# A two-layer decoder trunk in fp32: in the second layer's attention, the copies of a head's transposed probabilities and its value product come one head later, and ScalarE writes the longer high parts

## The chip, the cores and the metric

The kernel runs on one core of a Trainium2 chip. Five engines work side by side, each through its own queue in order: TensorE (PE in the profile, its weight loads apart as PEld), VectorE (DVE), ScalarE (ACT), GpSimd (POOL) and SyncE (SP), which issues the DMAs. The metric is the device time of one launch in microseconds; smaller is better. Beside the timed runs there is one profiled execution, from which all rows of the profile come.

## The reference, cut to what matters

512 positions with 1024 features pass through two layers, each an attention mixer and a squared-ReLU MLP. The change lies in the mixer of the second layer, the forgetting attention with 16 heads of 64 features:

```python
def fox_mixer(h, w_in, b_forget, w_out):
    q, k, v, fz = _split(h @ w_in, ODD_SPLITS)      # 16 heads x 64 each, and 16 forget logits
    log_f = jax.nn.log_sigmoid(fz + b_forget)
    cum = jnp.cumsum(log_f, axis=1).transpose(0, 2, 1)
    def block(c):                                   # 128 queries
        s = einsum('bhqd,bhkd->bhqk', qc, k) * scale + cq[..., None] - cum[:, :, None, :]
        p = masked_softmax(s, key_pos[None, :] <= t[:, None])
        return einsum('bhqk,bhkd->bhqd', p, v)
    ...
    return o @ w_out
```

All of it is in float32. Each head has four query blocks of 128 rows; block qi sees 128 x (qi + 1) keys.

## The kernel before, in words

**Products.** TensorE works on numbers in two parts: a high part in a rounded float32 format and a low part, the rest. A product of two such numbers takes three matmuls (`mm3`, lines 129 to 131: high by high, high by low, low by high). For every loaded piece of a weight, ACT writes the high part into the tile `whl` (line 91) and DVE or POOL subtracts it from the raw weight (line 94). A string of letters, `FOX_LOW`, tells for each piece of this stage which of the two engines subtracts: 34 letters, D for DVE, P for POOL.

**The stage.** `fox` runs through a written list of steps:

```python
FOX_ORDER = "v0 f k0 k1 k2 k3 p0 v1 k4 p1 p2 o01 k5 v3 v2 p3 k6 p4 p5 p6 k7 o23 o45 p7 o67"
```

`v` computes the values of four heads, `f` the sums of the forget logits, `k3` the queries and keys of pair 3 (heads 6 and 7), `p3` the attention of this pair, `o23` the output projection of pairs 2 and 3 with the addition to the residual stream. The list is the order in which the program is written. The order on each engine comes from a scheduler that plays the program through with modelled durations; work in a priority block (`self.prio()`) is taken ahead of work written earlier. A pool with n buffers lets a tile begin only when the tile n places before it was read to the end. Accumulators have two buffers for each name: `acc` for projections, `s` for logits, `o` for value products.

**Queries and keys.** A projection of 128 columns serves two heads and lies in `acc`. For each head ACT copies the query or key (lines 1259 and 1262), DVE computes the low part straight from `acc` (402 and 400) and POOL rounds a copy (406). The buffer of `acc` is free when both heads of the pair have been read out.

**One head in `softmax_t`.** The blocks are taken in two halves, first queries 3 and 2, then 1 and 0. For each block TensorE makes the logits (line 457, two matmuls), DVE adds the mask and takes the row's bound (461), ACT takes the exponent and its row sum (462). For each half DVE computes the two scales of its rows (464, 465). Then the scaled probabilities are written as float16 into the tile `HL`, the high part by POOL (472) and the low part by DVE (473), in pieces of 384 and 128 columns (query 3), 384 (query 2), 256 and 128 (queries 1 and 0). SP issues one transposing DMA from `HL` to `HT` (475). ACT copies the high half of `HT` into `PTh` (479) and POOL the low half into `PTl` (through `round`, 406). TensorE multiplies with the values (`pv`, 489 and 490), and `combine` scales the result into one half of the pair's tile `o` (ACT at 499, DVE at 500). After both heads of a pair POOL splits `o` into two parts `O` (`split_o`, 406 and 505). The output projection works on the two pairs' `O` (129 to 131), and DVE adds each of its eight accumulators to the residual (520).

**Buffers.** The probabilities `P` have three (`fP`), `HL` two, `HT` one, `PTh` and `PTl` two each.

The functions as they stand before the change:

Of the kernel before, what the change touches and what calls it, by code (L numbers as in the profile page):

```python
# [7 lines left out]
F32 = mybir.dt.float32  # L8
# [3 lines left out]
AF = mybir.ActivationFunctionType  # L12
ALU = mybir.AluOpType
AX = mybir.AxisListType

P = 128
S = 512
D = 1024
NT = S // P
# [8 lines left out]
P_UP = 32768.0  # L28
# [20 lines left out]
class Trunk:  # L49
# [395 lines left out]
    def softmax_t(self, passes, band):  # L445


        nc = self.nc
        pt = self.pP.tile([P, PTW], F32, tag="P", name=self.nm("P"))
        st = self.sm.tile([P, 3, 4], F32, tag="sst", name=self.nm("sst"))  # L450
        hl = self.pHL.tile([P, 2, PTW], F16, tag="HL", name=self.nm("HL"))
        for q0 in (2, 0):
            for qi in (q0 + 1, q0):
                w = P * (qi + 1)
                ps = self.psum("s")
                for i, (q, k) in enumerate(passes):
                    nc.tensor.matmul(ps[:, :w], q[:, qi * P:(qi + 1) * P], k[:, :w],
                                     start=i == 0, stop=i == len(passes) - 1)
                seg = pt[:, SEG[qi]:SEG[qi] + w]
                mn, sm = (st[:, a, qi:qi + 1] for a in range(2))  # L460
                nc.vector.tensor_tensor_reduce(seg, ps[:, :w], band[:, S - w:S], 1.0, 3e38, ALU.add, ALU.min, mn)
                nc.scalar.activation(seg, seg, AF.Exp, bias=mn, scale=-1.0, accum_out=sm)
            r = st[:, 2, q0:q0 + 2]
            nc.vector.reciprocal(r, st[:, 1, q0:q0 + 2])
            nc.vector.tensor_scalar(r, r, P_UP, None, op0=ALU.mult)
            for qi in (q0 + 1, q0):
                r = st[:, 2, qi:qi + 1]
                parts = [(0, min(qi + 1, 3), qi * P)] + ([(3, 4, PTOFF[3])] if qi == 3 else [])
                for j0, j1, off in parts:
                    seg = pt[:, SEG[qi] + j0 * P:SEG[qi] + j1 * P].rearrange("p (j c) -> p j c", c=P)  # L470
                    view = lambda a: hl[:, a, off:].rearrange("p (j c) -> p j c", c=P)[:, 0:3 * (j1 - j0 - 1) + 1:3, :]
                    nc.gpsimd.tensor_scalar(view(0), seg, r, 1.0, op0=ALU.mult, op1=ALU.mult)
                    nc.vector.scalar_tensor_tensor(view(1), seg, r, view(0), op0=ALU.mult, op1=ALU.subtract)  # L473
        t = self.pHT.tile([P, 2 * PTW // P, P], F16, tag="HT", name=self.nm("HT"))
        nc.sync.dma_start_transpose(t, hl.rearrange("p a b -> p (a b)"))
        tv = t.rearrange("p (a b) c -> p a (b c)", a=2)
        hi = self.pPT.tile([P, PTW], FR, tag="PTh", name=self.nm("PTh"))
        lo = self.pPT.tile([P, PTW], FR, tag="PTl", name=self.nm("PTl"))
        nc.scalar.activation(hi, tv[:, 0], AF.Copy)
        self.round(lo, tv[:, 1])  # L480
        return hi, lo

    def pv(self, po, pt, vs, first, last):
# [688 lines left out]
    def fox(self, hs):  # L1172
        self.phase, self.pieces = FOX_LOW, 0
        nc, I = self.nc, self.I
        w = I["odd_w_in"][0]
        wo = I["odd_w_out"][0]
        lo, hi = slice(0, HD), slice(HD, P)
        with ExitStack() as cx:
            pool = lambda name, bufs: cx.enter_context(self.tc.tile_pool(name=name, bufs=bufs))
            self.pP = pool("fP", 3)  # L1180
            self.pPT = pool("fPT", 2)
            self.pHL = pool("fHL", 2)
            self.pHT = pool("fHT", 1)
            o2 = pool("fo", 2)
            a1 = cx.enter_context(self.tc.tile_pool(name="attf1", bufs=1))
            wv = self.cols(w, [(2048, 2304), (3072, 3088)])
# [2 lines left out]
            band = a1.tile([P, S], F32, name="mband")  # L1189
# [7 lines left out]
            V = [a1.tile([P, 16, 2, HD], FR, tag=f"v{t}", name=f"v{t}") for t in range(NT)]  # L1197

            def values(c):

                wc = wv if c == 0 else self.cols(w, [(2048 + 256 * c, 2304 + 256 * c)])
                for t in range(NT):
                    ps = self.psum("acc")
                    self.proj_n(ps, wc, 272 if c == 0 else 256, x, t)
                    if c == 0:
                        nc.vector.tensor_copy(zt[:, t], ps[:, 256:272])
                    dst = V[t][:, 4 * c:4 * c + 4]
                    with self.tc.high_priority(offset=0):
                        pv = ps[:, :256].rearrange("p (h d) -> p h d", h=4)
                        nc.scalar.activation(dst[:, :, 0, :], pv, AF.Copy)  # L1210
                        self.sub(dst[:, :, 1, :], pv, dst[:, :, 0, :])
# [30 lines left out]
            def qk(i):  # L1242
                wc = self.cols(w, [(128 * i, 128 * i + 128)])
                psq = self.psum("acc")
                self.proj_t(psq, wc, 0, x)
                wc = self.cols(w, [(1024 + 128 * i, 1024 + 128 + 128 * i)])
                psk = self.psum("acc")
                self.proj_t(psk, wc, 0, x)
                st = []
                for j, r in enumerate((lo, hi)):  # L1250
                    head = 2 * i + j
                    q1 = pq.tile([P, S], FR, tag="Q1", name=self.nm("Q1"))
                    q2 = pq.tile([68, S], FR, tag="Q2", name=self.nm("Q2"))
                    k1 = pq.tile([P, S], FR, tag="K1", name=self.nm("K1"))
                    k2 = pq.tile([68, S], FR, tag="K2", name=self.nm("K2"))
                    nc.sync.dma_start(q2[64:68].bitcast(F32), fd[head, 0:4])
                    nc.sync.dma_start(k2[64:68].bitcast(F32), fd[head, 4:8])
                    with self.tc.high_priority(offset=0):
                        nc.scalar.activation(q1[lo], psq[r], AF.Copy, scale=-SCALE)
                        self.round(q2[lo], q1[lo].bitcast(F32))  # L1260
                        self.sub(q1[hi], psq[r], q1[lo], -SCALE)
                        nc.scalar.activation(k1[lo], psk[r], AF.Copy)
                        self.round(k1[hi], k1[lo].bitcast(F32))
                        self.sub(k2[lo], psk[r], k1[lo])
                    st.append((q1, k1, q2, k2))
                return st

            def pair(i, st):
                o = o2.tile([P, S], F32, tag="o", name=self.nm("o"))
                for j in range(2):  # L1270
                    head = 2 * i + j
                    q1, k1, q2, k2 = st[j]
                    with self.prio():
                        pt = self.softmax_t([(q1, k1), (q2, k2)], band)
                        po = self.psum("o")
                        self.pv(po, pt, [self.flat(V[t][:, head]) for t in range(NT)], True, True)
                        self.combine(po, o, j == 0, 1.0 / P_UP)
                return self.split_o(o)

            st, o = {}, {}  # L1280

            def step(op, arg):
                if op == "v":
                    values(int(arg))
                elif op == "f":
                    forget()
                elif op == "k":
                    st[int(arg)] = qk(int(arg))
                elif op == "p":
                    o[int(arg)] = pair(int(arg), st[int(arg)])  # L1290
                elif op == "o":
                    pairs = [int(a) for a in arg]
                    self.out_proj(wo, pairs, [o[a] for a in pairs], hs)

            for s in FOX_ORDER.split():
                step(s[0], s[1:])
# [41 lines left out]
```

## Time and profile before

| | us |
|---|---|
| median of 3 runs | 1250.22 (1249.81 to 1255.96) |
| the profiled execution | 1252.43 |
| its span, first to last instruction | 1250.7 |
| PE busy | 1207.5 (97%) |
| PEld busy | 1015.8 (81%) |
| DVE busy | 989.8 (79%) |
| ACT busy | 652.2 (52%) |
| POOL busy | 505.2 (40%) |
| mean granted clock of TensorE | 0.986 of full speed |

The first mixer runs to about 290 us, the first MLP to 635, the forgetting attention to 900, and the second MLP to the end. How to read the rows: a group is a line, an engine, an operation and output<-inputs with their shapes, then the count, the busy time and the mean of one in ns, and the idle time just ahead of them with what ended it. A wait is put down to the instruction or DMA that came last. A row of windows gives the length, then for PE, PEld, DVE, ACT and POOL the busy time, then the clock that TensorE was granted, the busy share of the DMA engines and their GB/s. The chain of waits goes back from the last instruction to what released each step; a row of it has its start, its length and the instruction.

### The profile page before, as it was taken

To read this page: it belongs to the slowest core of one execution; us is meant where nothing else is said; L and a number is where in the kernel's file an instruction comes from. 1 tells how busy PE (TensorE), PEld (TensorE's weight loads), DVE (VectorE), ACT (ScalarE), POOL (GpSimd) and SP (SyncE) were. 2 spreads that over 40 slices of the span, in tenths; PEclk is the share of its full clock that TensorE was granted. 3 is DMA by queue.
4 is the path that set the end of the run, shared out by engine and by line. 5 is a ranking of instruction groups with operands and counts; after the bars stand their busy time and mean duration, and the time that the engine had idled before them with its cause. 6 is when DMAs were issued, how large, how long until landed. Compare 5 with 4: busy or idle time off the path is not lost.

```text
span 1250.7 us, 16964 instructions
## 1 busy us (share of the span) xinstructions
PE 1207.5 (97%) x6055; PEld 1015.8 (81%) x6055; DVE 989.8 (79%) x1683; ACT 652.2 (52%) x1163; POOL 505.2 (40%) x518
## 2 busy tenths in 40 slices
PE   9999999999999999999999898897899999999997
PEld 7889987888888888888887786886698888888886
DVE  7877778788887898789776788649587897789875
ACT  6447656774645445544345565455365445444542
POOL 3435466642533323332015756445335233332314
PEclk9999999999999999999999999998899999999999
DMA  8952232223333333332044554534454224333301
GB/s 243 338 158 55 81 116 71 62 91 98 111 113 101 106 95 103 114 105 82 5 111 110 131 116 94 128 105 83 137 144 125 85 85 135 101 90 96 101 1 68
DMA packets 183440, 134.25 MB, mean 107 GB/s; under 512 B 47875, under 2 KB 158635, under 8 KB 183356
## 3 DMA queue, kind: packets, MB, share of 16 engines
q1 hardware_dynamic: 183196, 132.94, 37.9%
q8 instruction: 48, 0.79, 0.3%
q14 instruction: 36, 0.29, 0.1%
q10 hardware_dynamic: 160, 0.23, 0.1%
HBM read 120.27 MB, written 7.64 MB: 102 GB/s over the span
## 4 chain that ended last, share of the span: by engine, by line
PE 83%; DVE 8%; DMA 4%; ACT 3%; issue 2%; POOL 1%; ACTq 0%; DVEq 0%; POOLq 0%; SPq 0%
PE acc L129 16%; PE acc L131 15%; PE acc L130 15%; PE s L1113 12%; PE o L1113 6%; DMA HT<-HL 4%; PE pt L1113 3%; PE s L417 2%; DVE HL L473 2%; PE pt L439 2%; PE o L489 1%; PE o L490 1%; DVE whl L94 1%; DVE x L520 1%; PE s L130 1%
## 5 line engine op out<-in xcount | busy, mean ns | idle before, releaser
L131 PE MATMUL acc<-xhi,whl 128*128 128x512 f32 (+1 forms) x768 | 295.7, 385 | 1.3 <-POOL whl L94 0.8
L129 PE MATMUL acc<-xhi,whl 128*128 128x512 f32 (+1 forms) x768 | 295.0, 385 | 1.0 <-DVE Q L402 0.8
L130 PE MATMUL acc<-xlo,whl 128*128 128x512 f32 (+1 forms) x768 | 294.0, 383 | 0.0
L94 DVE TENSOR_TENSOR whl<-raw,whl 128x1024 fp32r<-128x1024 f32 (+2 forms) x110 | 165.0, 1504 | 85.5 <-ACT whl L91 73.3
L1016 POOL TENSOR_TENSOR r<-r,yrow 128x512 f32<-128x512 f32 x64 | 97.9, 1529 | 318.0 <-ACT r L1015 315.6
L131 PEld LDWEIGHTS acc<-xhi,whl 128*128 128x128 f32 x768 | 145.3, 189 | 30.7 <-DVE whl L94 1.6
L91 ACT ACTIVATE whl<-raw 128x1024 fp32r<-128x1024 f32 (+1 forms) x139 | 144.9, 1047 | 46.4 <-PE acc L131 31.6
L129 PEld LDWEIGHTS acc<-xhi,whl 128*128 128x128 f32 x768 | 145.1, 189 | 29.0 <-PE acc L131 0.8
L1113 PE MATMUL s<-whl,sp 128*128 128x512 f32 x672 | 167.6, 390 | 0.0
L130 PEld LDWEIGHTS acc<-xlo,whl 128*128 128x128 f32 x768 | 145.6, 190 | 27.0
L1113 PEld LDWEIGHTS s<-whl,sp 128*128 128x128 f32 x672 | 126.2, 188 | 26.5
L1068 DVE TENSOR_TENSOR whl<-w,whl 128x1024 fp32r<-128x1024 f32 x98 | 134.9, 1378 | 8.6 <-ACT whl L1067 8.6
L1067 ACT ACTIVATE whl<-w 128x1024 fp32r<-128x1024 f32 x98 | 103.6, 1060 | 71.5 <-PE s L1113 43.7
L1015 ACT ACTIVATE r<-acc 128x512 f32<-128x512 f32 x62 | 37.1, 598 | 117.3 <-PE acc L131 117.3
L94 POOL TENSOR_TENSOR whl<-raw,whl 128x1024 fp32r<-128x1024 f32 x29 | 70.9, 2447 | 53.5 <-ACT whl L91 52.4
L1113 PE MATMUL o<-whl,sp 128*128 128x512 f32 x336 | 88.8, 391 | 0.0
L1073 DVE TENSOR_TENSOR w<-w,w 128x1024 f32<-128x1024 f32 x56 | 82.0, 1464 | 0.9
L1121 DVE TENSOR_TENSOR x<-s,x 128x512 f32<-128x512 f32 x112 | 74.8, 679 | 3.0 <-PE s L1113 3.0
L1113 PEld LDWEIGHTS o<-whl,sp 128*128 128x128 f32 x336 | 63.3, 188 | 13.6
L129 PE MATMUL acc<-whl,O 128*128 128x512 f32 x128 | 56.1, 440 | 14.6 <-DVE x L520 8.7
L400 DVE TENSOR_TENSOR sp<-act,sp 128x512 fp32r<-128x512 f32 x64 | 69.4, 1106 | 0.6 <-ACT sp L1024 0.6
L1018 ACT ACTIVATE act<-r 128x512 f32<-128x512 f32 x64 | 40.5, 633 | 45.4 <-POOL r L1016 45.3
(290 smaller groups left out, 2498.7 us busy)
## 6 DMA issues: line engine op xcount, KB each, us to landing
raw<-in_mlp_w SPq DMA_DIRECT2D x72, 512.0 KB
w<-in_mlp_w SPq DMA_DIRECT2D x56, 512.0 KB
raw<-in_odd_w_in SPq DMA_DIRECT2D x22, 512.0 KB
raw<-in_even_w_in SPq DMA_DIRECT2D x20, 512.0 KB
band<-bias_dram SPq DMA_DIRECT2D x24, 256.0 KB
bias_dram<-bias_rows SPq DMA_DIRECT2D x16, 320.0 KB
raw<-in_even_w_out SPq DMA_DIRECT2D x8, 512.0 KB
raw<-in_odd_w_out SPq DMA_DIRECT2D x8, 512.0 KB
```

The costliest lines, as they stand in the source:

```text
L91: nc.scalar.activation(hl[:, 0, :n], raw[:, :n], AF.Copy)
L94: eng.tensor_tensor(hl[:, 1, :n], raw[:, :n], hl[:, 0, :n].bitcast(F32), op=ALU.subtract)
L129: mm(ps, ahl[0], bhl[0], start=first, stop=False)
L130: mm(ps, ahl[0], bhl[1], start=False, stop=False)
L131: mm(ps, ahl[1], bhl[0], start=False, stop=last)
L400: self.nc.vector.tensor_tensor(out, ps, hi.bitcast(F32), op=ALU.subtract)
L1016: nc.gpsimd.tensor_tensor(r, r, row, op=ALU.mult)
L1067: nc.scalar.activation(t[:, 0], src, AF.Copy)
L1068: nc.vector.tensor_tensor(t[:, 1], src, t[:, 0].bitcast(F32), op=ALU.subtract)
L1073: nc.vector.tensor_tensor(out, a_, b_, op=op)
L1113: mm = lambda l, r, first, last: nc.tensor.matmul(ps, l, r, start=first, stop=last, skip_group_check=True)
L1121: nc.vector.tensor_tensor(hv, ps, hv, op=ALU.add)
```

## The change

The second half of `softmax_t` becomes a function of its own, `turned`: it makes `PTh` and `PTl` from `HT`. The caller runs `softmax_t` of a head first, and then, for the head before it, `turned`, the value product and `combine` (`behind`); the last head's turn comes when the last output projection asks for its pair. Two ties hold the copies in their engines' order: `PTh` is issued after the newest exponent on ACT, `PTl` after the newest high part that POOL wrote. `HT` gets a second buffer and `P` loses its third. For the first half of a head (queries 3 and 2: pieces of 384, 128 and 384 columns) ACT writes the high part, with the scale of the row, in place of POOL; POOL keeps the pieces of 256 and 128 columns of the second half. That is 48 instructions that change engines in the 16 heads.

In rows that show the order of instructions a name such as `PTh_1213_8012` is a tile with its number; the numbers differ between the two kernels. `whl` is a weight's two parts, `raw` the loaded weight, `Q1`, `Q2`, `K1`, `K2` the tiles of queries and keys, `s` the logits.

```diff
--- before.py
+++ after.py
@@ -459,7 +459,7 @@
                 seg = pt[:, SEG[qi]:SEG[qi] + w]
                 mn, sm = (st[:, a, qi:qi + 1] for a in range(2))
                 nc.vector.tensor_tensor_reduce(seg, ps[:, :w], band[:, S - w:S], 1.0, 3e38, ALU.add, ALU.min, mn)
-                nc.scalar.activation(seg, seg, AF.Exp, bias=mn, scale=-1.0, accum_out=sm)
+                self.p_act = nc.scalar.activation(seg, seg, AF.Exp, bias=mn, scale=-1.0, accum_out=sm)
             r = st[:, 2, q0:q0 + 2]
             nc.vector.reciprocal(r, st[:, 1, q0:q0 + 2])
             nc.vector.tensor_scalar(r, r, P_UP, None, op0=ALU.mult)
@@ -469,15 +469,25 @@
                 for j0, j1, off in parts:
                     seg = pt[:, SEG[qi] + j0 * P:SEG[qi] + j1 * P].rearrange("p (j c) -> p j c", c=P)
                     view = lambda a: hl[:, a, off:].rearrange("p (j c) -> p j c", c=P)[:, 0:3 * (j1 - j0 - 1) + 1:3, :]
-                    nc.gpsimd.tensor_scalar(view(0), seg, r, 1.0, op0=ALU.mult, op1=ALU.mult)
+                    if q0 == 2:
+                        nc.scalar.activation(view(0), seg, AF.Copy, scale=r)
+                    else:
+                        self.p_pool = nc.gpsimd.tensor_scalar(view(0), seg, r, 1.0, op0=ALU.mult, op1=ALU.mult)
                     nc.vector.scalar_tensor_tensor(view(1), seg, r, view(0), op0=ALU.mult, op1=ALU.subtract)
         t = self.pHT.tile([P, 2 * PTW // P, P], F16, tag="HT", name=self.nm("HT"))
         nc.sync.dma_start_transpose(t, hl.rearrange("p a b -> p (a b)"))
+        return t
+
+    def turned(self, t):
+
+
         tv = t.rearrange("p (a b) c -> p a (b c)", a=2)
         hi = self.pPT.tile([P, PTW], FR, tag="PTh", name=self.nm("PTh"))
         lo = self.pPT.tile([P, PTW], FR, tag="PTl", name=self.nm("PTl"))
-        nc.scalar.activation(hi, tv[:, 0], AF.Copy)
-        self.round(lo, tv[:, 1])
+        with self.tc.issue_after(self.p_act.ins):
+            self.nc.scalar.activation(hi, tv[:, 0], AF.Copy)
+        with self.tc.issue_after(self.p_pool.ins):
+            self.round(lo, tv[:, 1])
         return hi, lo
 
     def pv(self, po, pt, vs, first, last):
@@ -1177,10 +1187,10 @@
         lo, hi = slice(0, HD), slice(HD, P)
         with ExitStack() as cx:
             pool = lambda name, bufs: cx.enter_context(self.tc.tile_pool(name=name, bufs=bufs))
-            self.pP = pool("fP", 3)
+            self.pP = pool("fP", 2)
             self.pPT = pool("fPT", 2)
             self.pHL = pool("fHL", 2)
-            self.pHT = pool("fHT", 1)
+            self.pHT = pool("fHT", 2)
             o2 = pool("fo", 2)
             a1 = cx.enter_context(self.tc.tile_pool(name="attf1", bufs=1))
             wv = self.cols(w, [(2048, 2304), (3072, 3088)])
@@ -1265,17 +1275,28 @@
                     st.append((q1, k1, q2, k2))
                 return st
 
+            todo = []
+
+            def behind():
+
+                head, t, ot = todo.pop()
+                with self.prio():
+                    pt = self.turned(t)
+                    po = self.psum("o")
+                    self.pv(po, pt, [self.flat(V[t][:, head]) for t in range(NT)], True, True)
+                    self.combine(po, ot, head % 2 == 0, 1.0 / P_UP)
+                if head % 2:
+                    o[head // 2] = self.split_o(ot)
+
             def pair(i, st):
-                o = o2.tile([P, S], F32, tag="o", name=self.nm("o"))
+                ot = o2.tile([P, S], F32, tag="o", name=self.nm("o"))
                 for j in range(2):
-                    head = 2 * i + j
                     q1, k1, q2, k2 = st[j]
                     with self.prio():
-                        pt = self.softmax_t([(q1, k1), (q2, k2)], band)
-                        po = self.psum("o")
-                        self.pv(po, pt, [self.flat(V[t][:, head]) for t in range(NT)], True, True)
-                        self.combine(po, o, j == 0, 1.0 / P_UP)
-                return self.split_o(o)
+                        t = self.softmax_t([(q1, k1), (q2, k2)], band)
+                    if todo:
+                        behind()
+                    todo.append((2 * i + j, t, ot))
 
             st, o = {}, {}
 
@@ -1287,9 +1308,11 @@
                 elif op == "k":
                     st[int(arg)] = qk(int(arg))
                 elif op == "p":
-                    o[int(arg)] = pair(int(arg), st[int(arg)])
+                    pair(int(arg), st[int(arg)])
                 elif op == "o":
                     pairs = [int(a) for a in arg]
+                    if pairs[-1] not in o:
+                        behind()
                     self.out_proj(wo, pairs, [o[a] for a in pairs], hs)
 
             for s in FOX_ORDER.split():
```

## The prediction

> **What bounds the kernel now.** I read the chain that ended last first, then the windows of the stage the diff touches, then who waited for whom in it. The page's line of the chain:
>
> ```profile
> PE 83%; DVE 8%; DMA 4%; ACT 3%; issue 2%; POOL 1%; ACTq 0%; DVEq 0%; POOLq 0%; SPq 0%
> ```
>
> TensorE sets the end, so a microsecond is won or lost only where TensorE waits or runs slowly. The touched stage is layer 1's attention, about 660 to 900 us. The next rows are windows: length, then busy us of PE, PEld, DVE, ACT, POOL, then granted clock. The first is the whole stage, the others are eight places in it that I call P1 to P8.
>
> ```profile
> 660.00:900.00 240.00, 212.79 (x1059) 177.83 (x1058) 169.74 (x377) 119.63 (x238) 133.16 (x157) 0.94 0.47 107
> 676.00:686.00 10.00, 8.13 (x30) 6.17 (x30) 8.99 (x25) 5.29 (x14) 7.69 (x10) 0.83 0.64 108
> 696.00:706.00 10.00, 7.03 (x23) 5.11 (x23) 8.01 (x23) 4.96 (x12) 9.42 (x11) 0.83 0.45 114
> 717.00:728.00 11.00, 8.09 (x52) 6.63 (x51) 9.13 (x23) 8.85 (x20) 8.24 (x11) 1.00 0.33 94
> 752.00:760.00 8.00, 4.92 (x18) 3.50 (x17) 7.87 (x10) 3.58 (x6) 5.05 (x6) 0.79 0.54 126
> 785.00:798.00 13.00, 9.71 (x61) 8.81 (x60) 4.44 (x12) 5.59 (x10) 7.23 (x8) 0.87 0.71 168
> 845.00:860.00 15.00, 10.64 (x35) 8.20 (x35) 13.41 (x33) 7.50 (x18) 8.92 (x12) 0.77 0.37 80
> 872.00:884.00 12.00, 8.93 (x29) 6.98 (x29) 8.33 (x17) 2.25 (x4) 6.21 (x9) 0.72 0.40 113
> 889.00:899.00 10.00, 5.96 (x21) 3.84 (x20) 3.75 (x6) 4.19 (x5) 5.55 (x4) 0.84 0.25 75
> ```
>
> TensorE idles 240 - 212.79 = 27.2 us, and the clock costs 0.06 x 240 = 14.4 us more: 41.6 us is all that can be won here. Each place loses its idle time and its length times the missing clock: 3.6, 4.7, 2.9, 4.8, 5.0, 7.8, 6.4, 5.6 us, together 40.8. So a stall is paid about one and a half times: idle, then a slow window.
>
> In the sentence that follows stands a page's rule against the second payment. The Trainium skill, "TensorE: Matmul & The Clock Gate", Part 1, lets the clock fall after an idle window of about 3.4 us; here P1 idles 1.9 us in all and still shows 0.83, so the measurement decides.
>
> Who holds TensorE in the stage (us, times, longest), all rows over 1 us:
>
> ```profile
> PE acc L129 <- DVE x L520: 6.6, 5, 3.4
> PE acc L129 <- DVE Q L402: 4.7, 6, 2.5
> PE s L457 <- DVE sst L461: 4.2, 7, 1.1
> PE o L489 <- ACT PTh L479: 3.3, 3, 1.7
> PE acc L129 <- POOL O L406: 2.8, 1, 2.8
> PE acc L130 <- DVE whl L94: 1.9, 1, 1.9
> PE acc L129 <- DVE K L400: 1.9, 2, 1.3
> PE s L457 <- POOL K L406: 1.8, 1, 1.8
> ```
>
> Only 3.3 us wait for the copies by name. But the copies stand in the in-order queues of ACT and POOL and wait there for the transpose's landing:
>
> ```profile
> L406 POOL TENSOR_SCALAR PTl<-HT x16: 1254/1261/1613, 690.1 to 889.2; 128x1280 fp32r<-128x1280 f16 x16
> L479 ACT ACTIVATE PTh<-HT x16: 1255/1272/1280, 690.4 to 889.1; 128x1280 fp32r<-128x1280 f16 x16
>   DMA HT<-HL: 52.9, 24
> ```
>
> That is 52.9 us of idle queues in 24 waits, with the Q and K copies that free TensorE's accumulators queued behind. The chain of waits (start, us, what) shows this twice, ahead of P4 and at P5:
>
> ```profile
> 742.01 4.93 DMA HT<-HL
> 747.32 1.27 ACT PTh L479
> 750.45 0.49 ACT Q L1259
> 754.36 0.69 DVE Q L402
> ...
> 783.48 4.92 DMA HT<-HL
> 789.78 0.59 ACT K L1262
> 791.97 0.70 DVE K L400
> ```
>
> A landing takes 4.9 us, the copy 1.27, and the Q or K copy leaves only then.
>
> **The change, part by part.** Work on TensorE is the same; only idle and slow time can move.
>
> The first piece of the new order is ACT around P5 (PTh is the copy, Q1/K1 free accumulators, whl is a weight's high part). Before:
>
> ```order
> L1259 ACTIVATE Q1_1131_7462<-acc_1127_7407 64x512
> L91 ACTIVATE whl_1142_7493<-raw_1140_7488 128x1024
> L1259 ACTIVATE Q1_1135_7474<-acc_1127_7407 64x512
> L479 ACTIVATE PTh_1213_8012<-HT_1212_8010 128x1280
> L1262 ACTIVATE K1_1133_7464<-acc_1130_7437 64x512
> L91 ACTIVATE whl_1149_7608<-raw_1147_7604 128x1024
> L1262 ACTIVATE K1_1137_7476<-acc_1130_7437 64x512
> ```
>
> Now:
>
> ```order
> L488 ACTIVATE PTh_1210_7997<-HT_1197_7938 128x1280
> L509 ACTIVATE o_1151_7704<-o_1200_7944 64x512
> L1269 ACTIVATE Q1_1127_7444<-acc_1123_7389 64x512
> L91 ACTIVATE whl_1138_7475<-raw_1136_7470 128x1024
> L1269 ACTIVATE Q1_1131_7456<-acc_1123_7389 64x512
> L1272 ACTIVATE K1_1129_7446<-acc_1126_7419 64x512
> L91 ACTIVATE whl_1145_7590<-raw_1143_7586 128x1024
> L1272 ACTIVATE K1_1133_7458<-acc_1126_7419 64x512
> ```
>
> The copy between Q and K is gone; the one ahead of Q reads a transpose of the head before, while TensorE still has the Q projection to do. At P5 I leave 1.0 of 5.0 us: -4.0. At P4 the same cause goes (2.5 of its 3.1 us idle, and the slow window), but the out-projection that follows shares accumulators with a K projection still unread; I leave 2.5 of 4.8: -2.3. At P2 I take nothing: heads 0 and 1 run interleaved, both transposes are issued back to back, and the copy of head 0 stands behind one exponent of head 2 only, still before the landing. The extremes for P2 are 0 and its 4.7.
>
> The second piece is the end, on POOL. Before:
>
> ```order
> L406 TENSOR_SCALAR PTl_1324_8581<-HT_1322_8578 128x1280
> L94 TENSOR_TENSOR whl_1340_8706<-raw_1339_8704,whl_1340_8706 128x1024
> L406 TENSOR_SCALAR O_1326_8595<-o_1303_8486 128x512
> L505 TENSOR_TENSOR O_1326_8595<-o_1303_8486,O_1326_8595 128x512
> ```
>
> Now:
>
> ```order
> L406 TENSOR_SCALAR PTl_1324_8581<-HT_1319_8563 128x1280
> L406 TENSOR_SCALAR O_1326_8595<-o_1299_8468 128x512
> L515 TENSOR_TENSOR O_1326_8595<-o_1299_8468,O_1326_8595 128x512
> L94 TENSOR_TENSOR whl_1340_8706<-raw_1339_8704,whl_1340_8706 128x1024
> ```
>
> The MLP's first weight no longer stands ahead of the last O. Rows of the timeline of DVE and POOL (start, us) price this and the place before it:
>
> ```profile
> 868.68 0.34 DVE L473 SCALAR_TENSOR_TENSOR HL<-P,sst,HL 128x128 f16<-128x128 f32 x1
> 870.48 3.45 DVE L94 TENSOR_TENSOR whl<-raw,whl 128x1024 fp32r<-128x1024 f32 x1
> ...
> 870.47 2.38 POOL L94 TENSOR_TENSOR whl<-raw,whl 128x1024 fp32r<-128x1024 f32 x1 [2.99 <-ACT whl L91]
> 892.40 2.42 POOL L94 TENSOR_TENSOR whl<-raw,whl 128x1024 fp32r<-128x1024 f32 x1 [1.93 <-ACT whl L91]
> 894.80 0.62 POOL L406 TENSOR_SCALAR O<-o 128x512 fp32r<-128x512 f32 x1
> ```
>
> At P8 2.4 us of POOL work leave the chain in front of O, and six more matmuls of the out-projection stand behind the last value product instead of ahead of it. I keep the wait for the last landing (it has no later head to hide behind) and take 3.0 of 5.6: -2.6. At P7 the DVE subtract started beside POOL's and took 3.45 us, 2.38 of them with POOL; now DVE's row stands earlier, since the weight's high part is made as soon as the old pair's buffer is free. I halve it: 6.4 to 3.4, -3.0 (0 if the two meet again). At P6 the residual add of the out-projection moves ahead of a pair of HL writes in DVE's order, so the 3.4 us wait shortens: 7.8 to 4.5, -3.3 (0 if not).
>
> The third piece is TensorE at P3. Now:
>
> ```order
> L457 MATMUL s_1092_7225<-K2_1000_6685,Q2_998_6683 128x128
> L457 MATMUL s_1101_7259<-K1_1003_6696,Q1_1001_6694 128x512
> L457 MATMUL s_1101_7259<-K2_1004_6697,Q2_1002_6695 128x512
> L457 MATMUL s_1102_7264<-K1_1003_6696,Q1_1001_6694 128x384
> L457 MATMUL s_1102_7264<-K2_1004_6697,Q2_1002_6695 128x384
> L457 MATMUL s_1103_7277<-K1_1003_6696,Q1_1001_6694 128x256
> L457 MATMUL s_1103_7277<-K2_1004_6697,Q2_1002_6695 128x256
> L457 MATMUL s_1104_7282<-K1_1003_6696,Q1_1001_6694 128x128
> L457 MATMUL s_1104_7282<-K2_1004_6697,Q2_1002_6695 128x128
> L457 MATMUL s_1155_7708<-K1_1013_6768,Q1_1011_6766 128x512
> ```
>
> Six logit tiles in a row, through two banks that DVE empties; before, value products and projections stood between them. Two waits of the longest size so far (1.1) join, and one slow window of 1.7 (0.17 x 10, as in P2) may follow; the K wait of 1.3 at P3 goes. 2.2 + 1.7 - 1.3 with half an addition for the rest: +1.8 net after 0.8 for the removed product wait at this place. P1 gets one tile more in its row: +0.5.
>
> The longer high parts go from POOL to ACT. Groups by form (busy, mean ns, idle before), of the old writer, the DVE partner and ACT's nearest kin:
>
> ```profile
> L472 POOL TENSOR_SCALAR HL<-P,sst 128x384 f16<-128x384 f32 x32 | 23.7, 741 | 27.6 <-ACT P L462 13.3 <-DVE sst L465 11.8 <-DVE sst L464 2.5
> L472 POOL TENSOR_SCALAR HL<-P,sst 128x128 f16<-128x128 f32 x32 | 11.9, 373 | 0.0
> L473 DVE SCALAR_TENSOR_TENSOR HL<-P,sst,HL 128x384 f16<-128x384 f32 x32 | 24.7, 772 | 3.3 <-POOL HL L472 3.3
> L473 DVE SCALAR_TENSOR_TENSOR HL<-P,sst,HL 128x128 f16<-128x128 f32 x32 | 21.6, 676 | 0.0
> L462 ACT ACTIVATE P<-P,sst 128x384 f32<-128x384 f32 x16 | 9.7, 606 | 3.0 <-DVE sst L461 2.9
> L462 ACT ACTIVATE P<-P,sst 128x128 f32<-128x128 f32 x16 | 6.3, 396 | 16.1 <-DVE sst L461 15.9
> ```
>
> POOL loses 32 x 0.741 + 16 x 0.373 = 29.7 us. ACT gains 16 x (2 x 0.606 + 0.396) = 25.7 us, and the wait for the scales: of POOL's 27.6 us idle, the 13.3 for the exponent vanish (same engine) and 14.3 come along. So 40 us join an engine that is busy 119.6 of 240 and loses most of its 52.9 us share of landings: it fits, but each head puts 2.5 us in front of the Q and K copies behind it. I charge 3.0 us, between 0 and 20 (8 pairs x 2.5, all reaching TensorE). DVE gains: its short write takes 0.34 alone and 0.676 on average, and POOL runs next to it less: up to 32 x 0.336 = 10.8 us. I count none beyond P6 and P7.
>
> One probability buffer fewer makes the exponent input of head h+2 wait for head h's last HL write; DVE's order has it so anyway, and I put it inside P3's term. SP's transposes keep their places among the loads to within a few rows: 0.
>
> Sum: -4.0 - 2.3 - 2.6 - 3.0 - 3.3 + 1.8 + 0.5 + 3.0 = -9.9 us. The profiled execution took 1252.4 (span 1250.7), 2.2 above the median of the runs shown; so 1242.5 on its scale, **1240.3** on that of the median.
>
> **Rivals.**
> (a) The landing is still waited for: the two heads of a pair interleave, so "one head later" is a few rows, as at P2. P4 and P5 keep their loss: -9.9 + 6.3 = -3.6, 1246.6. For it: P2's order. Against: the piece shown at P5.
> (b) The logit rows are the new bound: four of eight pairs in rows like P3's, 8 x 1.1 = 8.8 less the 1.8 counted, +7.0: 1247.3. For it: 4.2 us of such waits now, and two longer rows in the new order. Against: the other pairs' tiles are spread as before.
> (c) The slow windows stay although the idle time shrinks, since their rhythm is not the length of a stall: only idle time is won, 9.9 x 27.2 / 41.6 = 6.5, 1243.7. The page named above would allow no slow window for any stall here, as the longest is 3.4 us, and would give this time too.
> (d) ScalarE becomes the clog, the slower side: the writes and their waits for the scales stand in front of Q and K copies. Full price 20 us against 9.9 - 3.0 + 3.0: +10, 1260. It decides once over half of the pairs' evictions are delayed their whole 2.5 us (10 us). For it: ACT waits in order on DVE. Against: half of ACT is free.
> (e) DVE's relief arrives: TensorE's waits for DVE are 6.6 + 4.7 + 4.2 + 1.9 + 1.9 of 27.2 us, and half of the 10.8 with two slow windows (3.4) gives 8.8 more: 1231.5.
>
> **How the numbers follow.** Forecast 0.48, own range 1235 to 1246; (a) 0.13, (b) 0.13, (c) 0.06, (d) 0.13, (e) 0.07. A difference under 0.5% (6.3 us) is about what a measurement here cannot tell from none. Faster by more: 0.42 of the forecast's 0.48, all of (e), 0.06 of the rest: 0.55. Slower: (d) and a little of (b): 0.14. Within: 0.31. The range 1231 to 1253 leaves out most of (d), whose charge for ScalarE has the widest bounds, and half of (e): 0.13, and a few hundredths at the ends of the others.
>
> **What would show it.** Right: ACT's and POOL's idle time for the landing falls from 52.9 to under 20; TensorE's waits on Q, K and PTh copies (4.7 + 1.9 + 1.8 + 3.3) fall by more than half; the clock of the stage reads 0.96; the last O waits under 1.5 us; the POOL group at 128x384 is gone and ACT's is near 0.6 us. Wrong: waits of TensorE on logit reads above 8 us (b), on Q and K above 15 (d), an unchanged landing wait (a), or a clock still at 0.94 with less idle time (c).

## The result

The changed kernel takes **1237.92 us** (1237.84 to 1239.53) against 1250.78 us (1249.81 to 1255.96): the ratio is 0.989, 95% interval 0.986 to 0.992, 12.9 us less. 1240.3 was predicted, range 1231 to 1253.

The page of the profiled execution (1239.53 us; span, then busy time and share of each engine):

```profile
span 1237.8 us, 16953 instructions
PE 1201.4 (97%) x6055; PEld 1011.2 (82%) x6055; DVE 986.7 (80%) x1683; ACT 672.7 (54%) x1211; POOL 481.3 (39%) x470
```

Windows of the stage: the first row holds the same 1059 matmuls as the row of 240.00 us before; the others are P1, P2, P3, P4, P5, P6, P7 and P8 in turn, now some us earlier or later (columns as in the prediction).

```profile
661.90:887.20 225.30, 206.39 (x1059) 173.31 (x1059) 165.58 (x376) 139.87 (x286) 109.04 (x109) 0.96 0.50 114
678.00:688.00 10.00, 8.54 (x38) 6.66 (x38) 9.43 (x30) 7.24 (x20) 6.35 (x8) 1.00 0.34 97
695.00:704.00 9.00, 6.17 (x28) 4.62 (x28) 8.63 (x21) 8.24 (x18) 3.99 (x7) 1.00 0.18 58
713.00:730.00 17.00, 12.98 (x60) 10.48 (x59) 15.44 (x41) 12.67 (x32) 12.01 (x14) 0.70 0.51 116
752.00:767.00 15.00, 12.52 (x53) 9.83 (x52) 12.17 (x26) 8.19 (x17) 6.18 (x7) 0.89 0.48 115
782.00:798.00 16.00, 15.39 (x107) 14.17 (x106) 10.91 (x25) 9.94 (x22) 10.07 (x12) 1.00 0.59 143
838.00:850.00 12.00, 10.84 (x55) 8.72 (x54) 11.33 (x37) 9.23 (x24) 6.52 (x8) 1.00 0.44 87
856.00:875.00 19.00, 14.38 (x62) 11.38 (x61) 17.67 (x35) 9.45 (x17) 11.49 (x10) 0.91 0.61 127
877.00:887.00 10.00, 8.81 (x38) 6.04 (x37) 5.74 (x8) 4.91 (x7) 6.48 (x4) 1.00 0.29 82
```

240.0 us have become 225.3, 14.7 less. Idle time fell from 27.2 to 18.9 us, and the same matmuls are busy 206.39 instead of 212.79 us because fewer of them run at the low clock. Both parts of the forecast's payment are there, 8.3 us of idle time and 6.4 us of clock. These are two single executions: over the timed ones the mean granted clock rose from 0.988 (19 of the kernel before, run beside the first experiments) to 0.991 (4 of the changed one), which is some 4 us of clock. One place is much worse, P3: 17 us with 4.0 idle and a clock of 0.70.

The whole span shrank by 12.9 and not 14.7 because TensorE stood 2.0 us later already at 63 us in this execution, in the first mixer. Up to 640 us all engines run the same instructions in the same order in both traces, so this is not the change. The second MLP took the same time in both.

Who holds TensorE in the same stretch (us, times, longest), and who waits for the transpose (idle us, times):

```profile
PE s L457 <- DVE sst L461: 5.1, 5, 1.7
PE acc L129 <- DVE x L530: 4.3, 3, 2.7
PE acc L129 <- DVE Q L402: 3.1, 4, 1.6
PE o L499 <- ACT PTh L488: 3.1, 3, 1.9
PE s L457 <- POOL K L406: 1.8, 2, 1.5
```

```profile
  DMA HT<-HL: 23.6, 10
  POOL PTl L406: 12.5, 4
  ACT PTh L488: 11.1, 6
```

The idle time for the landing went from 52.9 to 23.6 us. TensorE's waits for Q and K copies fell from 8.4 to 4.9 us, those for logit reads rose from 4.2 to 5.1, and the wait for the last O on POOL (2.8) is gone. With the copy `PTh` (3.3, now 3.1) the first group falls from 11.7 to 8.0 us, less than the half that the forecast set as a sign. The stage's clock of 0.96 is what it had set.

### The profile page after: what moved, and what is told of

Its sections match the earlier page's. It is cut to its first block, busy times and chain, and to the rows that moved or that the text cites. A ratio compares the mean times of both kernels' runs of the same rounds, so it can differ in the third digit from the quotient of the medians.

```text
span 1237.8 us, 16953 instructions
## 1 busy us (share of the span) xinstructions
PE 1201.4 (97%) x6055; PEld 1011.2 (82%) x6055; DVE 986.7 (80%) x1683; ACT 672.7 (54%) x1211; POOL 481.3 (39%) x470
## 4 chain that ended last, share of the span: by engine, by line
PE 61%; DVE 8%; ACT 2%; DMA 2%; issue 2%; POOL 1%; DVEq 0%; ACTq 0%; POOLq 0%
PE s L1123 12%; PE acc L131 11%; PE acc L129 11%; PE acc L130 11%; PE o L1123 6%; PE pt L1123 3%; DVE HL L476 2%; DMA HT<-HL 2%; DVE P L461 1%; DVE whl L94 1%; PE s L131 1%; PE s L130 1%; PE s L129 1%; PE s L457 1%; DVE x L530 1%
## 5 line engine op out<-in xcount | busy, mean ns | idle before, releaser
L94 DVE TENSOR_TENSOR whl<-raw,whl 128x1024 fp32r<-128x1024 f32 (+2 forms) x110 | 161.7, 1473 | 84.8 <-ACT whl L91 68.5
L1077 ACT ACTIVATE whl<-w 128x1024 fp32r<-128x1024 f32 x98 | 103.6, 1059 | 71.2 <-PE s L1123 43.5
L422 ACT ACTIVATE P<-P,sst 128x128 f32<-128x128 f32 (+1 forms) x96 | 53.3, 557 | 14.4 <-DVE sst L421 12.6
```

The costliest lines, as they stand in the source:

```text
L94: eng.tensor_tensor(hl[:, 1, :n], raw[:, :n], hl[:, 0, :n].bitcast(F32), op=ALU.subtract)
L1077: nc.scalar.activation(t[:, 0], src, AF.Copy)
```

## The experiments

All ratios are against the kernel before, run on the same chip beside them.

**The two halves of the change.** The delay alone keeps the new function and the ties, and POOL writes:

```diff
-                    if q0 == 2:
-                        nc.scalar.activation(view(0), seg, AF.Copy, scale=r)
-                    else:
-                        self.p_pool = nc.gpsimd.tensor_scalar(view(0), seg, r, 1.0, op0=ALU.mult, op1=ALU.mult)
+                    self.p_pool = nc.gpsimd.tensor_scalar(view(0), seg, r, 1.0, op0=ALU.mult, op1=ALU.mult)
```

> The change without ScalarE's writes: POOL writes all high parts again, the copies and the value product still come one head later, with the ties and the two transpose buffers. Theory of the prediction (the gain is that the copies no longer wait for the transpose's landing in front of the Q and K copies): most of the gain stays, 1238 to 1243 us against 1250.8 of before, and the idle time of ACT and POOL for the landing stays under 30 us (52.9 before, 23.6 with the whole change). Rival (the gain is that POOL is relieved and VectorE has the shared path for itself): 1247 to 1252 us, and VectorE's short low parts go back to 0.67 us.

Measured: 1240.0 us, ratio 0.991 (0.989 to 0.992), landing waits 17.1 us. VectorE's short low parts do go back to 0.70 us, and the gain stays all the same. The stage, from its first matmul to the last of its output projection, takes 14.1 us less than before in the profiled execution, where the whole change takes 14.8 less. The writes alone are the kernel before with `if q0 == 2: nc.scalar.activation(...)` around the high parts:

> The kernel before, and ScalarE writes the high parts of queries 3 and 2; no delay, one transpose buffer. Theory of the prediction: alone the writes only load ScalarE's queue ahead of the Q and K copies (my charge of 0 to 20 us for them, 3.0 taken), so no gain: 1250 to 1255 us, the landing still waited for about 50 us. Rival (relief of POOL and VectorE): 1240 to 1246 us.

Measured: 1249.5 us, 0.9986 (0.9977 to 0.9996), landing waits 57.9 us. So the delay gives 10.2 of the 12.9 us and the writes next to nothing by themselves. On top of the delay they may give 2.1 (1240.0 to 1237.9, with intervals that overlap). The delay brings buffers with it, a second `HT` and one `P` fewer; no run has these alone. The relief of POOL and VectorE is not the cause of the 10.2 us, and ScalarE does not clog.

**The ties.** The two `issue_after` blocks are taken out:

```diff
-        with self.tc.issue_after(self.p_act.ins):
-            self.nc.scalar.activation(hi, tv[:, 0], AF.Copy)
+        self.nc.scalar.activation(hi, tv[:, 0], AF.Copy)
```

and the same for `round`.

> The whole change without its two ties, so that the scheduler may take a copy ahead of the next head's exponents and high parts. In the new order 4 of the 16 copies on ACT then stand behind no exponent of the next head, as in the kernel before. If it is the place behind the next head that hides the landing: landing waits 35 to 50 us and 1241 to 1248 us. If writing the copies one head later in the program is enough: 1236 to 1240 us and waits near 24 us.

Measured: 1244.6 us, 0.994 (0.992 to 0.996), the lines of the view of the transpose's tile:

```profile
  DMA HT<-HL: 58.2, 19
  POOL PTl L406: 32.5, 8
  ACT PTh L487: 25.7, 11
```

More than half of the gain is lost. Writing the copies later in the program is not enough: the scheduler pulls some of them up again, and on ACT the wait for the landing comes back from 11.1 to 25.7 us (31.1 before the change). On ACT and POOL together it is 58.2 us, more than expected and more than before the change. What the ties do can be read at P5, in the timeline of ACT in this run:

```profile
792.63 1.27 ACT L487 ACTIVATE PTh<-HT 128x1280 fp32r<-128x1280 f16 x1 [3.64 <-DMA HT<-HL]
793.93 0.59 ACT L1270 ACTIVATE K<-acc 64x512 fp32r<-64x512 f32 x1
```

The copy stands between Q and K again, as in the kernel before. TensorE's waits at 780 to 800 us in the kernel before, and the only one in the changed kernel:

```profile
PE s L457 <- POOL K L406: 1.8, 1, 1.8
PE acc L129 <- DVE Q L402: 0.9, 1, 0.9
PE acc L129 <- DVE K L400: 0.5, 1, 0.5
```

```profile
PE acc L129 <- DVE Q L402: 0.6, 1, 0.6
```

Without the ties they are 1.7, 1.4 and 0.5 us at this place. This run keeps the buffers, the program order and the writes, and has 5.6 of the 12.9 us; the rest comes only with the ties.

**What holds the end (P8).** One subtraction of the second MLP's first weight goes from POOL to VectorE, by `"D"` in place of `MLP_LOW` in the last MLP. TensorE's order is the same.

> The kernel before with one instruction on another engine: the subtraction of the second MLP's first weight goes from POOL, where it stands ahead of the last O, to VectorE; TensorE's order is the same. If that 2.4 us subtraction is what the last out-projection waits for (place P8, 5.6 us lost): the wait of 2.8 us falls to under 1 and the slow window behind it goes, 2.5 to 4.5 us faster, 1246.3 to 1248.3. If the last landing and its copies set the time there: under 1 us.

Measured: 1250.3 us, 1.000 (0.998 to 1.002): nothing. The timelines there show why, first two rows of the kernel before, then this run, then the changed kernel:

```profile
889.14 1.27 ACT L479 ACTIVATE PTh<-HT 128x1280 fp32r<-128x1280 f16 x1 [5.24 <-DMA HT<-HL]
895.47 0.55 PE L129 MATMUL acc<-whl,O 128*128 128x512 f32 x1 [2.77 <-POOL O L406]
```

```profile
887.33 1.27 ACT L479 ACTIVATE PTh<-HT 128x1280 fp32r<-128x1280 f16 x1 [6.29 <-DMA HT<-HL]
888.51 1.99 ACT L91 ACTIVATE whl<-raw 128x1024 fp32r<-128x1024 f32 x2
889.58 2.36 DVE L94 TENSOR_TENSOR whl<-raw,whl 128x1024 fp32r<-128x1024 f32 x2 [2.20 <-ACT whl L91]
890.52 0.59 ACT L499 ACTIVATE o<-o 64x512 f32<-64x512 f32 x1
891.98 0.69 DVE L500 SCALAR_TENSOR_TENSOR o<-o,o 64x512 f32<-64x512 f32 x1
892.76 0.62 POOL L406 TENSOR_SCALAR O<-o 128x512 fp32r<-128x512 f32 x1 [4.10 <-DVE o L500]
```

```profile
877.30 1.27 ACT L488 ACTIVATE PTh<-HT 128x1280 fp32r<-128x1280 f16 x1 [2.36 <-DMA HT<-HL]
880.22 0.59 ACT L509 ACTIVATE o<-o 64x512 f32<-64x512 f32 x1 [1.64 <-PE o L500]
880.84 0.69 DVE L510 SCALAR_TENSOR_TENSOR o<-o,o 64x512 f32<-64x512 f32 x1 [1.66 <-ACT o L509]
880.91 2.01 ACT L91 ACTIVATE whl<-raw 128x1024 fp32r<-128x1024 f32 x2
881.62 0.62 POOL L406 TENSOR_SCALAR O<-o 128x512 fp32r<-128x512 f32 x1 [2.93 <-DVE o L510]
883.16 0.63 PE L129 MATMUL acc<-whl,O 128*128 128x512 f32 x2
```

From the copy's start to O it was 894.80 - 889.14 = 5.7 us before. With POOL's piece gone it is 892.76 - 887.33 = 5.4: the same weight's high parts still stand ahead of `combine` on ACT, and the subtraction now stands ahead of it on VectorE. In the changed kernel all three queues have the weight behind, and O starts 881.62 - 877.30 = 4.3 us after the copy. There are also twelve matmuls of the out-projection between the last value product and the first matmul that needs O, where three stood before. The first nine start every 0.23 us. In the changed kernel the twelve run from 880.02 to 883.16 us, and the high part of O is there at 881.62 + 0.62 = 882.24, in time. Before, the three ran from 891.85 us, and the high part was there at 895.42, with the wait of 2.77 us between. In the run of the delay alone, with six such matmuls and the weight ahead of O, a wait of 2.1 us is left. What the shorter queues and what the longer cover are worth was not tried apart.

**P3: the row of logits.** The logits of heads 4 and 5 alternate between the tags `s` and `pt`, so that four accumulators take turns instead of two:

```diff
-                ps = self.psum("s")
+                ps = self.psum("pt" if self.wide and qi % 2 == 0 else "s")
```

> The changed kernel, and the logits of heads 4 and 5 (place P3) go in turn into four accumulators instead of two (the two of the transposes, which are idle there, join them). The row of six logit tiles at P3 becomes one of four and one of two. If the row of logit tiles through two accumulators is what TensorE waits for at P3 (waits of 1.13 and 1.70 us on VectorE's bounds and three slow windows, some 8 of the 9.1 us lost there): 1230 to 1235 us against 1237.9, waits on logit reads under 3 us (5.1). If VectorE itself is late there (low parts that POOL's subtraction stretches, scales that wait for exponents): the same idle time comes up, 1236 to 1240 us.

Measured: 1233.5 us, 0.987 (0.984 to 0.989). P3 in this run, and the wait for logit reads in the whole stage:

```profile
712.00:728.00 16.00, 13.84 (x80) 12.61 (x79) 13.94 (x40) 14.38 (x36) 12.58 (x15) 0.89 0.67 147
PE s L457 <- DVE sst L461: 2.3, 3, 1.2
```

16 us now hold 80 matmuls, where 17 held 60, with 2.2 us idle and one slow window instead of three. So the loss at P3 was the row of logits. The order has this row of six tiles in the changed kernel and in its variants without ties, with all writes on ACT and with two transposes. The delay alone has no row over four and the writes alone none over five, so it takes both. The same for every head:

> The changed kernel with four logit accumulators for every head. The order gets rows of eight logit tiles at nine places. If the number of accumulators is the bound of the logits: 1229 to 1235 us. If VectorE's rate is (0.4 to 0.7 us for a tile beside low parts and evictions), longer rows only move the wait: 1237 to 1245 us with waits on logit reads above 5.1 us.

Measured: **1231.1 us**, 0.984 (0.982 to 0.986), the fastest of all kernels here, 6.8 us under the changed one. No wait for logit reads is left; copies of K and Q head the list:

```profile
661.30:878.10 216.80, 201.19 (x1058) 170.76 (x1057) 157.52 (x375) 138.92 (x285) 109.70 (x109) 0.98 0.51 124
PE acc L129 <- DVE K L400: 4.0, 3, 2.0
PE acc L129 <- DVE Q L402: 3.0, 3, 1.7
```

The clock of the stage is 0.98. The longest rows in this trace have four tiles of two matmuls each, not the eight tiles that the expectation names. That longer rows would only move the wait to VectorE's rate was wrong.

**Are the accumulators worth this without the delay?**

> The kernel before with four logit accumulators for every head, nothing else. If the accumulators' gain (6.8 us on top of the change) has nothing to do with the delay: 1242 to 1246 us. If it is the delay that puts the logits in a row and the accumulators only repair it: 1248 to 1252 us. The landing wait stays near 50 us in either case, since no copy is moved on purpose.

Measured: 1237.1 us, 0.990 (0.988 to 0.992). The kernel before gains 13.0 us from this one line, as much as from the whole change and 5 us more than the better of the two theories allowed. The landing wait, expected near 50 us, came out at 33.5. The two do not add: 12.9 and 13.0 apart, 19.3 together. Its view of the transpose:

```profile
  DMA HT<-HL: 33.5, 18
  ACT PTh L479: 24.5, 11
  POOL PTl L406: 9.0, 7
```

ACT still waits 24.5 us for landings, nearly as long as without the ties, and the kernel is 7.5 us faster than that run. One reading is that both edits give the landing time, by using it later or by making the logits sooner. That is argued from the sums and was not tried by itself.

**All high parts on ScalarE.**

```diff
-                    if q0 == 2:
-                        nc.scalar.activation(view(0), seg, AF.Copy, scale=r)
-                    else:
-                        self.p_pool = nc.gpsimd.tensor_scalar(view(0), seg, r, 1.0, op0=ALU.mult, op1=ALU.mult)
+                    self.p_pool = nc.scalar.activation(view(0), seg, AF.Copy, scale=r)
```

> The changed kernel with ScalarE writing all high parts, the pieces of 256 and 128 columns too: 14.4 us more on ACT, 16 us less on POOL. By my charge (a microsecond of writes in front of a pair's Q and K copies costs up to a microsecond): 16 x 0.9 us of writes, a quarter of it reaching TensorE: 1239 to 1243 us. If the charge for ScalarE is nothing, as the run of the writes alone says (-0.7 us): 1235 to 1238 us.

Measured: 1237.7 us, 0.990 (0.988 to 0.992), the changed kernel's time. Its groups of VectorE's low parts, ahead of those of the delay alone, where POOL writes all of them:

```profile
L473 DVE SCALAR_TENSOR_TENSOR HL<-P,sst,HL 128x384 f16<-128x384 f32 x32 | 22.2, 695 | 1.6 <-ACT HL L472 1.5
L473 DVE SCALAR_TENSOR_TENSOR HL<-P,sst,HL 128x128 f16<-128x128 f32 x32 | 13.2, 412 | 0.0
```

```profile
L473 DVE SCALAR_TENSOR_TENSOR HL<-P,sst,HL 128x384 f16<-128x384 f32 x32 | 24.9, 778 | 3.8 <-POOL HL L472 3.8
L473 DVE SCALAR_TENSOR_TENSOR HL<-P,sst,HL 128x128 f16<-128x128 f32 x32 | 22.4, 700 | 0.0
```

The relief is real: a short low part takes 0.41 instead of 0.70 us. The Trainium skill, "SBUF — State Buffer", section "Who interferes with whom", says that VectorE and GpSimd share a pair of ports under an exclusive lock, and these rows agree. The pieces of 256 columns don't share in it: 0.707 us here, 0.640 in the delay alone. So (700 - 412 + 778 - 695) x 32 ns = 11.9 us less 16 x 0.067 = 1.1, or 10.8 us of VectorE's time, bring TensorE 2.3 us at the most (1240.0 to 1237.7). The landing waits in this run are 62.5 us, 48.3 of them on POOL, and it is no slower for them. POOL is busy 92 of 230 us there.

**The landing by itself.** Each transposing DMA in two, high parts first:

```diff
-        nc.sync.dma_start_transpose(t, hl.rearrange("p a b -> p (a b)"))
+        for h in range(2):
+            nc.sync.dma_start_transpose(t[:, h * (PTW // P):(h + 1) * (PTW // P)], hl[:, h])
```

> The changed kernel with each head's transposing DMA split in two, high parts first, so that the copy on ACT can begin earlier. If what is left of the landing waits (23.6 us on ACT and POOL, 3.1 us of TensorE on the high copy) still costs time: landing waits under 15 us, 1234 to 1237 us. If the landing no longer matters: 1237 to 1240 us. If a transpose costs the same whatever its size (3.1 us on SP's queue for 20 blocks), the second half lands 3 us later and loads behind it too: 1239 to 1246 us.

Measured: 1236.2 us, 0.989 (0.986 to 0.992). It can't be told from the changed kernel, though a half takes 1.36 us of SP's queue against 3.1 for the whole. The landing waits stayed at 23.3 us, where the first theory asked for under 15; TensorE's wait on the high copy fell from 3.1 to 0.3. So the first two theories stay undecided, and the third, of a transpose that costs the same whatever its size, fell. The three variants on four accumulators:

> Four logit accumulators and each transposing DMA in two, high parts first. A half takes 1.36 us on SP's queue where a whole takes 3.1, so the high copy can begin earlier. If the last landings (2.5 us of TensorE's waits on the high copy) still cost time: 1227 to 1230 us. If not: 1230 to 1234 us.

Measured: 1232.6 us, 0.986 (0.984 to 0.987), with landing waits of 9.2 us: no gain on 1231.1.

> The changed kernel with four logit accumulators, but POOL writes all high parts again. By the runs so far ScalarE's writes are worth 2.1 us on top of the delay (1240.0 against 1237.9): 1232 to 1235 us against 1231.1. If that was only the fall of the slow windows: 1229 to 1232 us.

Measured: 1237.9 us, 0.991 (0.988 to 0.993): 6.8 us more than with ScalarE's writes, above both expectations. TensorE then waits 3.2 us for low copies on POOL, which are not in the list with the writes.

> The changed kernel with four logit accumulators, and the queries and keys of pair 5 are written ahead of the first output projection. Rows of eight logit tiles become fewer (six to four). If what is left of TensorE's waits (4.0 us on K, 3.0 on Q) comes from those rows: 1226 to 1230 us. If they only move: 1230 to 1234 us.

Measured: 1236.6 us, 0.990 (0.988 to 0.992), 5.5 us slower, with K waits of 4.1 and Q waits of 4.8 us. Each edit lets the scheduler rewrite the order of the whole stage, and moves of this size between runs that differ in other rows too can't be put down to the one edit. The comparisons that stand on more are those where a place shows the cause as well: the delay and the ties at P5, and the single heads at P3.

## Why the prediction was right, and by how much its steps were not

The time from a TensorE matmul of a projection to the same one further on gives what each place really changed against the trace of the kernel before (us). The borders lie where equally many logits and value products are done in both traces. The last column is the run of P8: but for one subtraction at 892 us it has the order of the kernel before on every engine, so up to there it shows how far one execution differs from another by itself.

| | predicted | measured | delay alone | order of before |
|---|---|---|---|---|
| P1, P2 | +0.5, 0 | -3.7 | -2.7 | -3.7 |
| P3 | +1.8 | +4.8 | +1.6 | +0.6 |
| P4 | -2.3 | -1.5 | -3.6 | +0.7 |
| P5 | -4.0 | -4.7 | -5.1 | -1.5 |
| P6 | -3.3 | -6.3 | -4.5 | -0.5 |
| P7 | -3.0 | +0.5 | +1.7 | -3.5 |
| P8 | -2.6 | -3.9 | -1.4 | +0.1 |
| charge for ScalarE | +3.0 | in the places | | |
| sum | -9.9 | -14.8 | -14.1 | -7.9 |

With the order of before the stage was 7.9 us shorter in that one execution, and the median of its launches is the same. So a place of one trace can move by up to 3.7 us with no cause in the program, and the terms can be checked only where they stand clear of the last column.

- **The mechanism** (copies that wait for a landing leave the queue ahead of the Q and K copies) was right at P5, where 5.0 us were lost and a single wait of 0.6 is left; without the ties the copy is back between Q and K and the place takes 0.4 us more than before. In the run of the delay alone P4 and P5 hold 8.8 of 14.1 us, in the whole change 6.2 of 14.8.
- **P4** gained less than said. A wait of the logits for a K copy on POOL (1.5 us) has come up there, and a slow window follows it.
- **P1 and P2** were predicted by their idle time, which did stay (1.5 and 2.8 us idle against 1.9 and 3.0). The clock stayed at 1.00 in both rows, where it had been 0.83. Nothing in the order foretells that (last section), and the order of before gives the same -3.7: this gain is luck.
- **P3** was named as the place that loses, for the right reason, and mis-sized: the two waits are 1.13 and 1.70 us as against 1.1 each, but three slow windows follow instead of one.
- **P8** came near its number, by another step. I gave the gain to the 2.4 us of POOL work that leaves the chain in front of O. Moved alone, that instruction is worth 0. In the changed kernel the weight left all three queues, and the cover grew by nine matmuls, not six.
- **P6 and P7.** At P6 the wait for the residual fell from 3.4 to 1.1 us and both slow windows went, more than said. P7 won nothing. Its wait for the subtraction (1.9 us) went as predicted, but a wait for a landing's copy (1.9) came in its place, and the one for the residual grew from 1.1 to 2.7.
- **The charge of 3.0 us for ScalarE** is the term most clearly wrong as a sum: -0.7 us with the writes alone, and no loss even with all high parts on ACT. The load came as worked out (25.6 us of writes and 13.3 of waits for scales, of the 40 predicted). What the writes cost on top of the delay is the row of logits at P3, where the delay alone loses 1.6 us and the whole change 4.8.
- **The rivals.** (a) fell: the pieces that were shown hold, though only thanks to the ties; without them it would have been half right. (b) is what happens at P3, one place and not four pairs. (c) did not hold, but less clearly than these two traces say: the half-speed windows of 3.41 us went from 9 to 5 in the stage, and the run with the order of before has 5 too. The timed launches put the clock at some 4 of the 12.9 us. (d) fell; its price counts the charge of 3.0 twice, for -9.9 - 3.0 + 20 = +7.1 would be 1257.3 us. (e) came with a small part: the short low parts went from 0.676 to 0.596 us, 32 x 0.08 = 2.6 us of VectorE's time.
- **The sign I had set** for the mechanism, landing waits under 20 us, was missed by a little (23.6) and is a poor one. 62.5 us cost nothing in one run. With the writes alone ACT waits 17.5 us and the time is 1249.5, with four accumulators and no delay ACT waits 24.5 us and the time is 1237.1. By these runs the sum of such waits does not order the times; what stands behind the waiting instruction has to be looked at.

That the sum came within 3 us of the measured 12.9 is in part luck: P3 and P7 were 3.0 and 3.5 us worse than said, P1 and P2 together, P6 and the charge 4.2, 3.0 and 3.0 us better. The forecast was best founded where an order row and a wait row named the same instruction (P5), and least where I priced one instruction out of a chain of three queues (P8).

## What to carry to other kernels

A copy that waits for a DMA in an in-order queue is best put behind the next unit of work, with a tie that keeps the scheduler from pulling it up again: without the ties more than half of the gain went. Before a wait is priced by the instruction that ends it, look for what comes to stand there when that instruction goes, on every queue of the chain. And when a row of one kind of tile waits for its readers, idle accumulators of another stage can be a cheap cure: one line gave as much here as the whole rearrangement. Before a place of one trace is explained, a run with the same order shows how far it moves by itself.

## What the runs showed of the hardware

The fall of TensorE's clock can be read as a rule on a fixed grid. In all 14 traces the clock changes in this stage lie 3.413 us or a multiple apart. Counted over the windows of this grid that ran at full clock: 31 windows had 1.85 us or more of idle time, and the next window was at half clock each time. 46 had 0.9 to 1.27 us, and it never was. Below 0.9 us it never was either. In between it was so in 13 of 51, and there the idle time alone does not tell: 1.28 us was followed by a slow window in the kernel before, 1.77 us in the run of P8 was not. The bounds were chosen on these same windows. A stall that a border of the grid divides so counts less in each of its windows. The same two stalls at P2, of 1.20 and 1.62 us, in the changed kernel and in the run with four accumulators at P3, three windows of the grid each:

```profile
694.20:697.62 3.42, 2.22 (x13) 1.66 (x12) 2.91 (x8) 3.40 (x8) 0.85 (x2) 1.00 0.06 12
697.62:701.03 3.41, 1.79 (x9) 1.28 (x8) 3.32 (x11) 3.38 (x8) 0.81 (x2) 1.00 0.47 154
701.03:704.44 3.41, 3.41 (x17) 2.80 (x16) 3.38 (x8) 2.26 (x6) 3.24 (x5) 1.00 0.00 0
```

```profile
692.89:696.30 3.41, 2.31 (x13) 1.71 (x11) 2.55 (x7) 3.36 (x8) 0.61 (x1) 1.00 0.29 56
696.30:699.71 3.41, 1.69 (x7) 1.23 (x8) 3.32 (x10) 3.38 (x9) 0.82 (x1) 1.00 0.49 154
699.71:703.12 3.41, 3.41 (x10) 2.64 (x9) 3.41 (x9) 2.94 (x7) 2.87 (x4) 0.50 0.00 0
```

1.62 us of idle time in the middle window leave the clock at 1.00, 1.72 us bring it to 0.50, and the third window does 10 matmuls instead of 17. A stall of about 1.5 us thus costs its own length or 1.7 us more (half of a window), and some of what a change seems to win or lose here is this: two such windows are 3.4 of the 3.7 us at P1 and P2, and they are gone in the run of P8 with the order of the kernel before. The Trainium skill, "TensorE: Matmul & The Clock Gate", Part 1, has the free-running window of the same length, but lets the clock fall only after a whole idle one; in this case half a window was enough.
